# The output projection as seven half-block products: one change to a tuned transformer layer on one core

## The chip, the cores and the metric

The kernel runs on one core of one Trainium2 chip. The metric is device microseconds of one execution. A core has TensorE (PE in the profile, its weight loads PEld), VectorE (DVE), ScalarE (ACT), GpSimd (POOL) and SyncE (SP, which here only issues transfers). Every transfer is issued from the queue of SP, ACT or POOL and is carried by 16 DMA engines that all queues share.

## The reference

One layer of an image generator, 1024 latent tokens of 1024 features, 256 context tokens, all in float32:

```python
h = rmsnorm(x, norm_g) * (1 + scale) + shift          # scale, shift, gate from the condition c
q, k, v, za, u, bg, cg, zc = split(h @ w_in)          # eight groups of 512 columns
attn = neighbourhood_attention(q, k, v, kc, vc, rpb) * silu(za)   # 8 heads, 8x16 window + 256 context keys
conv = bg * conv3(cg * u) * silu(zc)
out  = x + gate * (concat([attn, conv]) @ w_out)      # (1024 x 1024) @ (1024 x 1024)
```

The change concerns the last line, the output projection: y = concat([attn, conv]) has 1024 tokens by 1024 features and w_out is 1024 by 1024.

## The kernel before

Every large product is made in three passes: each float32 operand is split into a high part, rounded to float32r by a cast on ACT, and a low part, which DVE makes by subtracting the high part. TensorE then sums high·high, high·low and low·high (`mm3`, lines 88 to 92). Everything before the last stage keeps this pattern:

- A prologue normalises and modulates x and leaves it as eight blocks `hh`, `hl` of 128 features by 1024 tokens.
- The projection loop (n from 0 to 34, 32 steps with a token tile each, four head pairs of eight tiles) makes q, k and v in `pacc`. While it works on one head pair, SP loads the eight weight chunks (`wr`) of the next one, ACT casts them and DVE makes their low parts `w`; four of the eight are split in the first step of the new pair. In this stage the order of PE, ACT, DVE, POOL and SP is the order of the code (`strict`). Weights, spilled q, k and v, and gate weights all pass SP's queue, in order.
- Attention runs in quarters (`quarter`), four for each of eight heads. Between the score products, products of other columns (`pu`) fill TensorE. SP loads k into a buffer tagged A and q into one tagged B, in the pool `hcp` for even heads. Each finished head pair is gated and its y block is written to DRAM (`y_d`).
- The output projection. `put_y(f)` loads feature block f of y (two transfers from ACT's queue) and splits it into `yh`, `yl`. `load_wo(nh, f)` loads the 128x512 block of w_out for feature block f and column half nh and splits it into `woh`, `wol`. Feature blocks come in the order `FORDER` = 4, 5, 6, 0, 1, 2, 3, 7, as they become ready. y is the stationary operand (128 tokens as columns), w_out the moving one (512 output columns). Eight token tiles by two column halves make 16 output tiles, each a sum of 8 blocks by 3 passes, 24 matmuls. Six tiles of the first half are summed together, block by block, then the remaining ten one after the other; the last one is made in two pieces of 384 and 128 columns. Feature block 3 is the last attention block; it is gated here, out of `z_d`, `o_d` and the reciprocal sums, which POOL loads (`rb`).
- The gate: for the first half of the columns the output tile is multiplied by the gate row on DVE (line 1343) and the residual x is added on POOL (line 1344); for the second half the gate is multiplied into w_out before the split (line 1288), and one DVE addition out of PSUM makes the result (line 1340).

In the stage after attention `strict` is empty: a scheduler in the compiler orders each engine's instructions by its own estimate of when they can start.

Of the kernel before, what the change touches and what calls it, by code (L numbers as in the profile page):

```python
# [10 lines left out]
F32 = mybir.dt.float32  # L11
# [44 lines left out]
def body(tc, es, x, xb, xt, cb_, ct, w_mod, w_gate, b_ada, w_grp, w_col, q_g, k_g, bias, w_out, vecs, cst, out):  # L56
# [47 lines left out]
    def many(name, n, shape):  # L104
        return [dr.tile(shape, F32, name=f"{name}{i}")[:] for i in range(n)]
# [11 lines left out]
    v_d = many("v_d", NPAIR, [P, 2, NB + 2, HD])  # L117
    kc_d = many("kc_d", NPAIR, [P, 2, L])
    ri_d = many("ri_d", NPAIR, [2, T])


    cp = es.enter_context(sbuf("cp"))
# [45 lines left out]
    hcs = ExitStack()  # L168
    hcp = hcs.enter_context(sbuf("hcp"))
    hc = []  # L170

# [224 lines left out]
    def blocked(v):  # L396
        return v.rearrange("p (b r c) -> p b r c", b=2, r=16)
# [716 lines left out]
    tiles, scales, waiting, nxt, raws = {}, {}, [], [], []  # L1114
    NT = NPAIR * NB

    def flush():
# [91 lines left out]
    vs_ = ExitStack()  # L1209
    prp = vs_.enter_context(sbuf("prp"))  # L1210
    vts = [prp.tile([P, NB + 2, HD], F32, name=f"v{i}") for i in range(2)]

    gating = []

# [27 lines left out]
    with sbuf("att") as ap, psum("psb") as psb:  # L1242
# [6 lines left out]
        for n in range(len(TICKS)):  # L1249
# [24 lines left out]
        strict[:] = []  # L1274
    vs_.close()
    prs.close()
    hcs.close()


    op = es.enter_context(sbuf("op"))  # L1280
    pss = es.enter_context(psum("pso"))
    y, wo = {}, {}

    def load_wo(wp, nh, f):
        raw = op.tile([P, 512], F32, name="woraw", tag="woraw", bufs=4)
        act.dma_start(raw, w_out[0, f * P:(f + 1) * P, nh * 512:(nh + 1) * 512])  # L1286
        if nh:
            dve.tensor_tensor(raw, raw, gate[:, 512:], ALU.mult)
        wh = wp.tile([P, 512], F32R, name=f"woh{nh}{f}")
        wl = wp.tile([P, 512], F32R, name=f"wol{nh}{f}")  # L1290
        act.copy(wh, raw)  # L1291
        dve.tensor_tensor(wl, raw, wh[:].bitcast(F32), ALU.subtract)  # L1292
        wo[nh, f] = wh, wl

    def put_y(yp, f):

        yh = yp.tile([P, T], F32R, name=f"yh{f}")
        yl = yp.tile([P, T], F32R, name=f"yl{f}")
        for half in range(2):
            cols = slice(half * 512, (half + 1) * 512)  # L1300
            tb = yp.tile([P, 512], F32, name="tb", tag="zt", bufs=4 if yp is op else 2)
            if f == NPAIR - 1:
                zs = op.tile([P, 512], F32, name="zs", tag="zt", bufs=4)
                rb = op.tile([P, 512], F32, name="rb", tag="rb", bufs=2)
                act.dma_start(zs, z_d[f][:, cols])
                act.dma_start(tb, o_d[f][:, cols])
                load_sums(f, half, rb, pool)
                act.activation(zs, zs, AF.Silu)
                dve.tensor_tensor(zs, zs, rb, ALU.mult)
                dve.tensor_tensor(tb, tb, zs, ALU.mult)  # L1310
            else:
                act.dma_start(tb, y_d[f][:, cols])  # L1312
            tv = blocked(tb[:]) if f < NPAIR else by_row(tb[:])
            act.copy(natural(yh[:], half), tv)  # L1314
            dve.tensor_tensor(natural(yl[:], half), tv, natural(yh[:].bitcast(F32), half), ALU.subtract)  # L1315
        y[f] = yh, yl

    for f in FORDER[:-1]:
        put_y(op, f)
        load_wo(op, 0, f)  # L1320
    load_wo(op, 0, FORDER[-1])
    hs.close()
    rp = es.enter_context(sbuf("rp", side="right"))
    put_y(rp, FORDER[-1])
    gate = rp.tile([P, D], F32, name="gate")
    sp.dma_start(gate, g_d.broadcast_to([P, D]))

    def out_mm(ps, nh, t, f, c=slice(0, 512)):
        rows = slice(t * P, (t + 1) * P)
        mm3(ps[:, c], y[f][0][:, rows], y[f][1][:, rows], *(w[:, c] for w in wo[nh, f]), f == FORDER[0], f == FORDER[-1])  # L1330

    def out_tile(ps, nh, t, pieces=(slice(0, 512),)):
        rows, cols = slice(t * P, (t + 1) * P), slice(nh * 512, (nh + 1) * 512)
        xr = rp.tile([P, 512], F32, name="xr", tag="xr", bufs=3)
        sp.dma_start(xr, x[0, rows, cols])
        ot = rp.tile([P, 512], F32, name="ot", tag="ot", bufs=3)
        if nh:
            for c in pieces:
                part = slice(c.start + 512, c.stop + 512)
                dve.tensor_tensor(ot[:, c], ps[c.start][:, c], xr[:, c], ALU.add)  # L1340
                sp.dma_start(out[0, rows, part], ot[:, c])
        else:
            dve.tensor_tensor(ot, ps, gate[:, cols], ALU.mult)
            pool.tensor_tensor(ot, ot, xr, ALU.add)
            sp.dma_start(out[0, rows, cols], ot)

    first = {t: bank("pout", "SCO"[t // 2]) for t in range(6)}
    for f in FORDER:
        for t in first:
            out_mm(first[t], 0, t, f)  # L1350
    for f in FORDER:
        load_wo(rp, 1, f)
    for t in first:
        out_tile(first[t], 0, t)
    for n, (nh, t) in enumerate([(0, 6), (0, 7)] + [(1, t) for t in range(NB)]):
        pieces = [slice(0, 384), slice(384, 512)] if (nh, t) == (1, NB - 1) else [slice(0, 512)]
        ps = {c.start: bank("pout", "USC"[(n + i) % 2 + i]) for i, c in enumerate(pieces)}
        for c in pieces:
            for f in FORDER:
                out_mm(ps[c.start], nh, t, f, c)  # L1360
        out_tile(ps if nh else ps[0], nh, t, pieces)


def constants():
# [58 lines left out]
```

## Time and profile before

| what | value |
|---|---|
| time, median of 3 runs | 607.62 us (606.13 to 609.37) |
| profiled execution, its own time | 607.57 us |
| span in its profile | 605.6 us |
| PE busy | 592.9 us, 98% |
| DVE busy | 399.7 us, 66% |
| ACT busy | 273.0 us, 45% |
| POOL busy | 66.3 us, 11% |
| first matmul of the output projection | 512.79 us |
| last DVE instruction | 602.73 us, for 0.29 us |
| mean granted TensorE clock | 0.994 |

In a timeline row stand the start, the duration, the engine, the line, the operation, what is written out of what, its shape, a count, and in brackets how long the engine was idle before and what ended that. Rows with a count stand for several instructions in a row. A tile row gives the shortest, median and longest duration in nanoseconds. A windows row gives, for a stretch, the busy time of each engine with its count, the granted clock, the busy share of the DMA engines and GB/s.

### The profile page before, as it was taken

How to read it: one execution, taken by the hardware profiler on the slowest of the kernel's cores; microseconds unless marked ns; L12 is line 12 of the kernel's file. 1: busy time of each engine (PE TensorE's matmuls, PEld its weight loads, DVE VectorE, ACT ScalarE, POOL GpSimd, SP SyncE). 2: the span in 40 equal slices, each digit the busy share in tenths (PEclk: the TensorE clock that was granted, in tenths of full speed). 3: DMA queues.
4: the chain of work that ended last, by engine and by line, in shares of the span. 5: the costliest groups of instructions: out<-in, count | busy, mean ns of one | idle time of the engine just before them, and what ended most of it. 6: DMA issues, size and time to landing. Idle time of an engine off the chain costs nothing. (4 is left out here: it accounts for less than half of the span.)

```text
span 605.6 us, 9468 instructions
## 1 busy us (share of the span) xinstructions
PE 592.9 (98%) x3347; PEld 502.0 (83%) x3348; DVE 399.7 (66%) x833; ACT 273.0 (45%) x636; POOL 66.3 (11%) x86
## 2 busy tenths in 40 slices
PE   7799999999999999999999999999999999999998
PEld 3477899999999999888878787877878777778887
DVE  1475889745636645458989697999798884394201
ACT  6645446426525445434554464646446444360000
POOL 1001025123223221100000000000000002003300
PEclk9899999999999999999999999999999999999999
DMA  8995566733524764766162838274823218963731
GB/s 331 412 416 201 179 214 188 254 126 114 191 91 148 225 222 162 280 237 217 52 246 93 275 106 297 94 264 155 307 87 92 89 36 238 332 195 105 244 106 52
DMA packets 63227, 116.14 MB, mean 192 GB/s; under 512 B 7377, under 2 KB 26313, under 8 KB 60876
## 3 DMA queue, kind: packets, MB, share of 16 engines
q1 hardware_dynamic: 57860, 105.82, 50.7%
q10 hardware_dynamic: 5064, 9.18, 4.8%
q0 software_dynamic: 256, 0.54, 0.3%
q8 instruction: 26, 0.43, 0.3%
q14 instruction: 21, 0.17, 0.1%
HBM read 86.08 MB, written 29.43 MB: 191 GB/s over the span
## 5 line engine op out<-in xcount | busy, mean ns | idle before, releaser
L71 PE MATMUL pu<-h,uh 128*128 128x512 f32 x544 | 172.2, 398 | 0.5 <-ACT zs L71 0.5
L71 PE MATMUL pacc<-w,h 128*128 128x384 f32 x768 | 138.8, 337 | 0.9 <-ACT ub L71 0.5
L71 PEld LDWEIGHTS pacc<-w,h 128*128 128x128 f32 x768 | 132.7, 188 | 1.8 <-ACT ub L71 0.9
L71 PEld LDWEIGHTS pu<-h,uh 128*128 128x128 f32 x544 | 97.2, 188 | 19.3 <-issue 1.2
L71 PE MATMUL pu<-h,ul 128*128 128x512 f32 x272 | 106.6, 392 | 0.0
L71 PEld LDWEIGHTS pu<-h,ul 128*128 128x128 f32 x272 | 51.1, 188 | 11.6 <-DVE ul L71 0.2
L71 POOL TENSOR_TENSOR ss<-ss,few 128x4 f32<-128x4 f32 (+1 forms) x40 | 41.1, 1028 | 126.3 <-DVE ss L71 126.1
L91 PE MATMUL pout<-wol,yh 128*128 128x512 f32 (+2 forms) x136 | 51.4, 379 | 0.0
L90 PE MATMUL pout<-woh,yh 128*128 128x512 f32 (+2 forms) x136 | 50.0, 381 | 0.5 <-ACT yh L1314 0.5
L92 PE MATMUL pout<-woh,yl 128*128 128x512 f32 (+2 forms) x136 | 49.3, 380 | 0.0
L71 PE MATMUL acc<-h,w 128*128 128x512 f32 x144 | 38.8, 415 | 0.0
L71 ACT ACTIVATE sc<-sc 128x512 f32<-128x512 f32 x32 | 20.2, 632 | 36.2 <-DVE sc L71 36.1
L71 DVE TENSOR_REDUCE ss<-sq 128x4 f32<-128x260 f32 (+1 forms) x40 | 15.7, 393 | 28.5 <-ACT sq L71 28.4
L71 PEld LDWEIGHTS acc<-h,w 128*128 128x128 f32 x144 | 26.9, 196 | 8.7 <-ACT h L71 1.2
L71 ACT COPY mg<-pmx 128x256 f32<-128x256 f32 (+1 forms) x33 | 12.1, 366 | 48.3 <-issue 22.8
L71 ACT ACTIVATE sq<-pacc 128x256 f32<-128x256 f32 x32 | 12.4, 387 | 47.4 <-PE pacc L71 46.7
L71 DVE TENSOR_TENSOR sum<-sum,sb 128x372 f32<-128x372 f32 (+2 forms) x64 | 31.0, 485 | 2.7
L71 ACT ACTIVATE qn<-pacc,ss 128x64 f32<-128x64 f32 x128 | 30.0, 330 | 4.9 <-PE trA L71 2.5
L71 DVE TENSOR_TENSOR mx<-mx,sb 128x372 f32<-128x372 f32 (+2 forms) x64 | 30.9, 483 | 1.9
L90 PEld LDWEIGHTS pout<-woh,yh 128*128 128x128 f32 x136 | 25.6, 188 | 5.9 <-ACT yh L1314 1.3
L71 DVE TENSOR_TENSOR sb<-pss,bt 128x192 f32<-128x192 f32 (+3 forms) x48 | 27.6, 601 | 4.2 <-PE pss L71 4.0
L92 PEld LDWEIGHTS pout<-woh,yl 128*128 128x128 f32 x136 | 25.6, 188 | 5.1 <-DVE yl L1315 0.4
(141 smaller groups left out, 931.1 us busy)
## 6 DMA issues: line engine op xcount, KB each, us to landing
uraw<-in_w_col SPq DMA_DIRECT2D x34, 256.0 KB, 2.9
slab<-in_w_mod SPq DMA_DIRECT2D x8, 1024.0 KB, 9.6
q_d<-qs SPq DMA_DIRECT2D x32, 256.0 KB, 2.0
k_s<-k_d SPq DMA_DIRECT2D x8, 1024.0 KB, 8.3
q_s<-q_d SPq DMA_DIRECT2D x16, 512.0 KB, 6.0
wr<-in_w_grp SPq DMA_DIRECT2D x40, 192.0 KB, 3.0
bt<-in_rpb SPq DMA_DIRECT2D x8, 564.0 KB, 6.2
xn<-in_xb SPq DMA_DIRECT2D x8, 512.0 KB, 8.1
```

Source lines behind the costliest of these rows:

```text
L71: i = emit(*a, **kw)
L90: i = pe.matmul(ps, ah, bh, start=first, stop=False)
L91: pe.matmul(ps, ah, bl, start=False, stop=False)
L92: pe.matmul(ps, al, bh, start=False, stop=last)
```

## The change

The output projection is computed transposed, output columns on partitions and tokens along the free axis, by a scheme of Strassen's kind with seven products of half blocks in place of eight. w_out is cut in four blocks of 512 features by 512 columns, with the feature blocks 4, 5, 6, 0 in the first half and 1, 2, 3, 7 in the second (`K_HALVES`); y is cut in four blocks of 512 features by 512 tokens. A product has four column tiles of 128x512, each a sum of 4 feature blocks by 3 passes: 48 matmuls. The left operand (stationary) is a block of w_out or a sum of blocks, the right one (moving) a block of y or a sum of blocks.

- Sums of w_out: steps 9, 13, 17 and 21 of the projection loop load two 128x1024 rows of blocks of w_out each, steps 11, 15, 19 and 23 combine them by four DVE operations and write the two sums to DRAM (`w_d`). They are read back later, as left operands of products 3, 5, 6 and 7; products 1, 2 and 4 take w_out itself.
- The left operands of products 1 and 5 are loaded during attention, into the buffers A and B of `hcp`, which now stays open; the others follow into A and B in turn.
- y blocks are loaded whole (512 KB a transfer). Sums of y blocks are made by DVE (`combined`, 16 operations). Every operand is split by one ACT cast and one DVE subtraction (`split`, 56 of each). Operand buffers exist for 8 right and 6 left operands in each of two pools.
- Sums of products are taken in PSUM: products 6, 7 and 4 go on in the banks `a` in which product 1 was left. What must be kept from `a` before that, and from product 5, is scaled by the gate into an SBUF tile by ACT (`pg`, three buffers) and added by POOL to a residual tile `m` (12 times each). All other results are added into `m` by DVE with the gate as a scalar (`gated_add`), and stored. The residual comes from the transposed x, 16 tiles of 256 KB.

```diff
-FORDER = [4, 5, 6, 0, 1, 2, 3, 7]
+K_HALVES = [4, 5, 6, 0], [1, 2, 3, 7]
...
+    def load_blocks(i):
+        for fs in K_HALVES:
+            wsum.append(bmp.tile([P, 3 * 384], F32, name="ws", tag="bt", bufs=2)[:, :D])
+            sp.dma_start(wsum[-1], w_out[0, fs[i] * P:(fs[i] + 1) * P])
+
+    def add_blocks(i):
+        (a11, a21), (a12, a22) = ([v[:, :512], v[:, 512:]] for v in wsum)
+        dve.tensor_tensor(a22, a21, a22, ALU.add)
+        dve.tensor_tensor(a21, a11, a21, ALU.subtract)
+        dve.tensor_tensor(a11, a22, a11, ALU.subtract)
+        dve.tensor_tensor(a12, a12, a11, ALU.subtract)
+        for k in range(2):
+            spill(w_d[i][:, k], wsum.pop(0))
...
+        if 9 <= n < 25 and n % 4 == 1:
+            load_blocks((n - 9) // 4)
...
         do_dves()
+        if 9 <= n < 25 and n % 4 == 3:
+            add_blocks((n - 9) // 4)
...
+    def load_left(q, tag):
+        left_raw[q] = hcp.tile([P, 4, 512], F32, name="wraw", tag=tag)
+        for i in range(4):
+            sp.dma_start(left_raw[q][:, i], left_rows(q, i))
...
+            if n in (30, 31):
+                load_left(*((1, "A"), (5, "B"))[n - 30])
             quarter(n)
...
+    def split(pl, name, bufs, v, view):
+        two = pl.tile([P, 2, 512], F32R, name=name, tag=name, bufs=bufs)
+        hi, lo = view(two[:, 0]), view(two[:, 1])
+        act.copy(hi, v)
+        dve.tensor_tensor(lo, v, hi.bitcast(F32), ALU.subtract)
+        return two[:, 0], two[:, 1]
+
+    def combined(dst, v, w):
+        dve.tensor_tensor(blocked(dst[:]), v, w, ALU.subtract)
+        return blocked(dst[:])
...
+    def prepare(q, pl):
+        for i in range(4):
+            right[q, i] = split(pl, "right", 8, right_side(q, i), blocked)
+            left[q, i] = split(pl, "left", 6, left_raw[q][:, i], lambda v: v)
+
+    def product(q, ps, tiles_, steps, first=False, cols=slice(0, 512)):
+        for i in steps:
+            for c in tiles_:
+                (ah, al), (bh, bl) = left[q, i], right[q, i]
+                at = slice(c * P, (c + 1) * P)
+                for n, (a, b) in enumerate(((ah, bh), (ah, bl), (al, bh))):
+                    pe.matmul(ps[c][:, cols], a[:, at], b[:, cols], start=first and i == 0 and n == 0,
+                              stop=i == 3 and n == 2, skip_group_check=True)
...
+    def gated_copy(ps, c, m):
+        pg = rp.tile([P, 512], F32, name="pg", tag="pg", bufs=3)
+        act.activation(pg, ps, AF.Identity, scale=gcol[:, c:c + 1])
+        pool.tensor_tensor(m, m, pg, ALU.add)
+
+    def gated_add(ps, c, m, cols=slice(0, 512)):
+        dve.scalar_tensor_tensor(m[:, cols], ps[:, cols], gcol[:, c:c + 1], m[:, cols], ALU.mult, ALU.add)
...
+    a = four("SSCC")
+    c5 = four("OOUU")
+    product(1, a, every_tile, range(4), first=True)
+    for c in every_tile:
+        product(5, c5, [c], range(4), first=True)
+    m11 = [residual(c, 0) for c in every_tile]
+    for c in every_tile:
+        gated_copy(a[c], c, m11[c])
+    load_left(2, "A")
+    prepare(2, rp)
+    m12 = [residual(c, 1) for c in every_tile]
+    m22 = [residual(4 + c, 1) for c in every_tile]
+    for c in every_tile:
+        gated_copy(c5[c], c, m12[c])
+        gated_copy(c5[c], 4 + c, m22[c])
+    c2_ = four("OOUU")
+    product(2, c2_, every_tile, range(4), first=True)
+    load_left(6, "B")
+    prepare(6, rp)
+    for c in every_tile:
+        product(6, a, [c], range(4))
+        gated_add(c2_[c], c, m11[c])
+        put(m11[c], c, 0)
...
```

After product 6 come product 3 (banks O and U again), 7 and 4 (banks `a`) in the same manner; the last tile of product 4 is made in pieces of 384 and 128 columns.

The new instructions stand in the engines' order as follows. On DVE, in the projection loop where one head pair ends and the next begins (`ws` are the rows of w_out, `w` the low parts of weight chunks):

```order
 L71 TENSOR_TENSOR rtmp<-qn,rope 128x256
 L71 TENSOR_TENSOR rot<-rot,rtmp 128x8x16 x2
+L71 TENSOR_TENSOR ws<-ws 128x512 x4
 L71 TENSOR_TENSOR w<-wr,w 128x384 x4
 L71 TENSOR_REDUCE ss<-sq 128x4
```

Four operations now stand ahead of the low parts of the next pair's last four chunks, here and at the next change of pair.

On DVE, in the output projection, before the change, where feature blocks 1, 2 and 7 of y and the second half of w_out are split:

```order
L1315 TENSOR_TENSOR yl1_5593<-tb_5594,yh1_5592 128x2x16x16
L1292 TENSOR_TENSOR wol07_5659<-woraw_5656,woh07_5658 128x512
L1288 TENSOR_TENSOR woraw_5831<-woraw_5831,gate_5679 128x512
L1315 TENSOR_TENSOR yl1_5593<-tb_5598,yh1_5592 128x2x16x16
L1315 TENSOR_TENSOR yl2_5609<-tb_5610,yh2_5608 128x2x16x16
L1292 TENSOR_TENSOR wol14_5835<-woraw_5831,woh14_5834 128x512
```

and with the change, up to the operands of product 6's third feature block (`right_5947`, `left_5950`; 5955 is the fourth block's; 6034 and 6040 belong to product 3, 6109 to 6133 to product 7, the `t` are sums of y blocks):

```order
L1350 TENSOR_TENSOR right_6040<-y7_5668,right_6040 128x512
L1354 TENSOR_TENSOR t3_6131<-y7_5668,y0_5587 128x512
L1350 TENSOR_TENSOR right_6109<-t3_6107,right_6109 128x512
L1350 TENSOR_TENSOR right_6117<-t3_6115,right_6117 128x512
L1350 TENSOR_TENSOR right_5947<-t2_5945,right_5947 128x512
L1350 TENSOR_TENSOR right_5955<-t2_5953,right_5955 128x512
L1350 TENSOR_TENSOR right_6125<-t3_6123,right_6125 128x512
L1354 TENSOR_TENSOR t2_5945<-y3_5649,t2_5945 128x512
L1350 TENSOR_TENSOR left_5950<-wraw_5924,left_5950 128x512
```

Between DVE's first operand (`left_5592`, the first row after the gating of the last convolution's first half) and `left_5950` stand 58 rows, all but one of them with two SBUF inputs.

On ACT, before the change, the output projection holds only loads and casts:

```order
L1291 CAST woh15_5841<-woraw_5838 128x512
L1308 ACTIVATE zs_5627<-zs_5627 128x512
L1291 CAST woh16_5848<-woraw_5845 128x512
L1286 DMA woraw_5866<-in_w_out 128x512
L1308 ACTIVATE zs_5639<-zs_5639 128x512
L1291 CAST woh10_5855<-woraw_5852 128x512
```

and with the change the scaled copies `pg` out of the banks of product 1 (5679 to 5682) and product 5 (5683 to 5686) stand between the casts:

```order
L1415 ACTIVATE pg_5851<-pout_5683,gcol_5677 128x512
L1415 ACTIVATE pg_5854<-pout_5684,gcol_5677 128x512
L1349 CAST right_6034<-y3_5649 128x512
L1349 CAST right_6040<-y7_5668 128x512
L1349 CAST right_6109<-t3_6107 128x512
L1349 CAST right_6117<-t3_6115 128x512
L1349 CAST right_5947<-t2_5945 128x512
L1415 ACTIVATE pg_5857<-pout_5684,gcol_5677 128x512
L1349 CAST right_5955<-t2_5953 128x512
L1349 CAST right_6125<-t3_6123 128x512
L1415 ACTIVATE pg_5860<-pout_5685,gcol_5677 128x512
L1349 CAST left_5950<-wraw_5924 128x512
```

`pg_5860` is the ninth of the twelve copies and stands one row ahead of the cast of `left_5950`; POOL's addition of each copy follows it.

More of the change, by code (lines that the diff above doesn't have):

```diff
@@ L1295, in put_y, with load_y @@
-    def put_y(yp, f):
-        yh = yp.tile([P, T], F32R, name=f"yh{f}")
-        yl = yp.tile([P, T], F32R, name=f"yl{f}")
+    raw_y, t1, t2 = {}, {}, {}
+    def load_y(f, queue):
+        raw_y[f] = op.tile([P, 2, 512], F32, name=f"y{f}")
+        if f != NPAIR - 1:
+            queue.dma_start(raw_y[f][:].rearrange("p a n -> p (a n)"), y_d[f])
+            return
         for half in range(2):
+            tb = raw_y[f][:, half]
             cols = slice(half * 512, (half + 1) * 512)
[L1301 to L1321, printed above, removed]
+            zs, rb = (op.tile([P, 512], F32, name=n, tag=n, bufs=1) for n in ("zs", "rb"))
+            queue.dma_start(zs, z_d[f][:, cols])
+            queue.dma_start(tb, o_d[f][:, cols])
+            load_sums(f, half, rb, pool)
+            act.activation(zs, zs, AF.Silu)
+            dve.tensor_tensor(zs, zs, rb, ALU.mult)
+            dve.tensor_tensor(tb, tb, zs, ALU.mult)
+    def y_block(k, i, half):
+        f = K_HALVES[k][i]
+        return (blocked if f < NPAIR else by_row)(raw_y[f][:, half])
@@ L1322, in body @@
+    for f in K_HALVES[0]:
+        load_y(f, act)
+    prepare(1, op)
+    prepare(5, op)
+    for f in K_HALVES[1]:
+        load_y(f, act)
     hs.close()
     rp = es.enter_context(sbuf("rp", side="right"))
[L1324 to L1361, printed above, removed]
+    gcol = rp.tile([P, KT], F32, name="gcol")
@@ new lines, in body, with residual @@
+    sp.dma_start(gcol, g_d.rearrange("o (t p) -> p (o t)", p=P))
+    every_tile = range(4)
+    def residual(c, half):
+        m = rp.tile([P, 512], F32, name="m", tag="m", bufs=14)
+        sp.dma_start(m, xt[c, :, half * 512:(half + 1) * 512])
+        return m
+    def gated_copy(ps, c, m):
[4 more added lines that the diff above has]
+        dve.scalar_tensor_tensor(m[:, cols], ps[:, cols], gcol[:, c:c + 1], m[:, cols], ALU.mult, ALU.add)
@@ new lines, in put, with four @@
+    def put(m, c, half, cols=slice(0, 512)):
+        sp.dma_start(out[c, :, half * 512 + cols.start:half * 512 + cols.stop], m[:, cols])
+    def four(tags):
+        return [bank("pout", tag) for tag in tags]
+    a = four("SSCC")
[7 more added lines that the diff above has]
+    load_left(2, "A")
@@ new lines, in body @@
+    prepare(3, op)
+    c3 = four("OOUU")
+    for c in every_tile:
+        product(3, c3, [c], range(4), first=True)
+        gated_add(a[c], c, m12[c])
+    load_left(7, "B")
+    prepare(7, op)
+    for c in every_tile:
+        product(7, a, [c], range(4))
+        gated_add(c3[c], c, m12[c])
+        put(m12[c], c, 1)
+    load_left(4, "A")
+    prepare(4, rp)
+    m21 = [residual(4 + c, 0) for c in every_tile]
+    for c in every_tile:
+        gated_add(a[c], 4 + c, m22[c])
+        put(m22[c], 4 + c, 1)
+        if c < 3:
+            product(4, a, [c], range(4))
+            gated_add(a[c], 4 + c, m21[c])
+            put(m21[c], 4 + c, 0)
@@ L1364, in constants @@
+    head_, tail = slice(0, 384), slice(384, 512)
+    last = {3: bank("pout", "O")}
+    gated_add(a[3], 7, m21[3], tail)
+    product(4, a, [3], range(4), cols=head_)
+    product(4, last, [3], range(4), first=True, cols=tail)
+    gated_add(a[3], 7, m21[3], head_)
+    put(m21[3], 7, 0, head_)
+    gated_add(last[3], 7, m21[3], tail)
+    put(m21[3], 7, 0, tail)
 def constants():
```

45 lines of the change are left out of this document (30 added, 15 removed).

## The prediction

> **What bounds the kernel now.** I read the page's engine totals first, then the windows of the last hundred microseconds, then the timelines of TensorE and VectorE there. The page and the windows:
>
> ```profile
> PE 592.9 (98%) x3347; PEld 502.0 (83%) x3348; DVE 399.7 (66%) x833; ACT 273.0 (45%) x636; POOL 66.3 (11%) x86
> ```
>
> ```profile
> 510.00:520.00 10.00, 10.00 (x46) 8.29 (x45) 5.13 (x9) 3.81 (x7) 2.07 (x4) 1.00 1.02 268
> 520.00:530.00 10.00, 9.77 (x42) 7.45 (x42) 3.28 (x5) 2.91 (x6) 0.00 (x0) 1.00 0.97 357
> 530.00:540.00 10.00, 9.78 (x44) 7.77 (x43) 8.89 (x15) 6.58 (x12) 0.00 (x0) 1.00 0.69 222
> 540.00:550.00 10.00, 10.00 (x46) 8.28 (x45) 8.84 (x15) 4.53 (x8) 0.00 (x0) 1.00 0.24 71
> 550.00:603.00 53.00, 52.69 (x251) 44.68 (x249) 11.18 (x17) 0.00 (x0) 10.24 (x8) 1.00 0.42 143
> ```
>
> TensorE is the bound throughout, at full clock; in the output projection it is never short of work for more than 0.23 us in ten. VectorE is busy at 0.9 only from 530 to 550 and hardly after. How long a matmul takes when nothing is missing is read from VectorE's last additions, each of which is released by the 24 matmuls of its tile:
>
> ```profile
> 590.48 0.69 DVE L1340 TENSOR_TENSOR ot<-pout,xr 128x512 f32<-128x512 f32 x1 [4.75 <-PE pout L92]
> 595.92 0.69 DVE L1340 TENSOR_TENSOR ot<-pout,xr 128x512 f32<-128x512 f32 x1 [4.75 <-PE pout L92]
> 600.10 0.56 DVE L1340 TENSOR_TENSOR ot<-pout,xr 128x384 f32<-128x384 f32 x1 [3.49 <-PE pout L92]
> 602.73 0.29 DVE L1340 TENSOR_TENSOR ot<-pout,xr 128x128 f32<-128x128 f32 x1 [2.07 <-PE pout L92]
> ```
>
> 595.92 - 590.48 = 5.44 us for 24, 0.2267 us each; 4.18 / 24 = 0.174 us at 384 columns and 2.63 / 24 = 0.110 us at 128. The stage begins here:
>
> ```profile
> 512.79 1.75 PE L90 MATMUL pout<-woh,yh 128*128 128x512 f32 x7
> ```
>
> **What the change removes.** Before: 15 tiles of 24 at 0.2267 (81.6 us) and the last one (6.8 us) make 88.4 us of the 89.9 us from 512.79 to 602.73; 1.5 us are waits for operands. After: seven products of 48 matmuls, 324 at 0.2267 (73.5 us), 12 at 0.174 and 12 at 0.110 (3.4 us), 76.9 us. So TensorE has 11.5 us less to do, and if the old 1.5 us of waits went too, 13.0 us. What follows the last matmul (an addition of 128 columns and its store) keeps its form. Everything else is the question of new waits, S.
>
> **What it adds ahead of the stage.** In the projection loop VectorE gets 16 operations, four at a time. Two groups stand right ahead of the low parts of the next pair's last four chunks:
>
> ```profile
> 162.65 0.49 DVE L71 TENSOR_TENSOR rot<-rot,rtmp 128x128 f32<-128x128 f32 x2
> 163.06 1.96 DVE L71 TENSOR_TENSOR w<-wr,w 128x384 fp32r<-128x384 f32 x4
> ...
> 204.86 1.96 DVE L71 TENSOR_TENSOR w<-wr,w 128x384 fp32r<-128x384 f32 x4
> ...
> 535.42 0.68 DVE L1315 TENSOR_TENSOR yl<-tb,yh 128x512 fp32r<-128x512 f32 x1
> ...
> 538.43 0.68 DVE L1288 TENSOR_TENSOR woraw<-woraw,gate 128x512 f32<-128x512 f32 x1
> ```
>
> ```profile
> 158.96 8.60 PE L71 MATMUL pacc<-w,h 128*128 128x384 f32 x48
> ```
>
> Operations of 128x512 without a wait between them follow each other every 0.602 us (five steps from 535.42 to 538.43). Four of them, 2.4 us, move the first of these low parts from 163.6 to 166.0. TensorE has two tiles from 158.96 on, 0.179 us a matmul; the second starts at 163.3 and asks for that low part with its 14th matmul, at 165.6. Wait: 0.4 us, the later chunks follow faster than they are used. The second change of pair has the same row at 204.86; 0.8 us in all. At steps 11 and 19 no such low parts stand behind the group and VectorE idles soon after; nothing.
>
> SP's queue gets 16 transfers of 512 KB. A store waits for VectorE, the next load for that store, and chunk loads stand behind both. The last ones of the pair:
>
> ```profile
> 155.12 2.50 SPq L71 DMA_DIRECT2D wr<-in_w_grp  x2
> ```
>
> ```profile
> 160.53 2.23 ACT L71 CAST w<-wr 128x384 fp32r<-128x384 f32 x5
> ```
>
> The last is issued at 157.6 and cast at about 162.2, and TensorE needs its chunk at 163.3 + 21 x 0.179 = 167.0, so some 4 to 5 us of lateness are covered by work that TensorE has; two transfers of 512 KB at 268 GB/s take 4 us. I take nothing; if that cover is used up, up to 5 us at each of two changes of pair (a rival). In attention, the eight loads of the first left operands (2 MB) go ahead of a weight load at 448.57 whose cast runs at 456.43:
>
> ```profile
> 448.57 0.33 SPq L319 DMA_DIRECT2D uraw<-in_w_col  x1
> ```
>
> ```profile
> 456.43 0.60 ACT L71 CAST uh<-uraw 128x512 fp32r<-128x512 f32 x1
> ```
>
> At 300 GB/s (between the windows above) 1.5 MB ahead of it take 5 us; it still arrives. Nothing, bounded by 2 us.
>
> **What it adds in the stage: VectorE.** From the end of the gating of the last convolution's first half, VectorE runs a queue without a gap:
>
> ```profile
> 507.55 0.69 DVE L71 TENSOR_TENSOR cv<-pu,cv 128x512 f32<-128x512 f32 x1 [1.47 <-PE pu L71]
> 508.16 1.28 DVE L1315 TENSOR_TENSOR yl<-tb,yh 128x512 fp32r<-128x512 f32 x2
> ```
>
> The first row that TensorE waits for, the low part of the first y block, is the ninth: 508.16 + 9 x 0.602 = 513.6, asked for at 513.7 (four high·high matmuls go first). [...] The tight one is `left_5950`, the 58th row: 508.16 + 58 x 0.602 = 543.1. TensorE asks for it after products 1 and 5, two blocks of product 6, two tiles of product 2 and 8 matmuls, 152 in all: 512.79 + 152 x 0.2267 = 547.3. So the queue is 4.2 us early, if nothing stops it. What it reads comes in time by the old rows; the slowest are the reciprocal sums of block 3:
>
> ```profile
> 510.06 2.07 POOL L530 DMA_DIRECT2D rb<-ri_d  x4 [4.86 <-PE pu L71]
> ```
>
> ```profile
> DMA to landing us min/median/max: 7.1/8.0/9.0
> ```
>
> Issued at 510.06, landed by 520, read by the 22nd row, at 508.16 + 21 x 0.602 = 520.8. Lateness up to the 4.2 us in hand costs nothing.
>
> **What can stop it: POOL.** Twelve additions of 128x512 on POOL, with both inputs in SBUF, now fall into this queue: they need product 1 (ends at 512.8 + 10.9 = 523.7) and the residual tiles, which SP issues behind a load that waits for VectorE's 23rd row, 522.0, so they begin at about 530. Ahead of `left_5950` on ACT stand nine of the scaled copies, with three buffers; at least six additions, likely nine, run before it. What such an addition does to VectorE, the trace shows for smaller ones in the projection loop:
>
> ```profile
> L71 DVE TENSOR_TENSOR rot<-rot,rtmp x64: 277/291/554, 88.8 to 256.4; 128x128 f32<-128x128 f32 x64
> ```
>
> ```profile
> L71 POOL TENSOR_TENSOR kn<-kn,gkc x8: 481/578/912, 98.5 to 222.2; 128x128 f32<-128x128 f32 x8
> ```
>
> ```profile
> 221.97 0.91 DVE L71 TENSOR_TENSOR rot<-rot,rtmp 128x128 f32<-128x128 f32 x2
> ```
>
> ```profile
> 221.78 0.95 POOL L71 TENSOR_TENSOR kn<-kn,gkc 128x128 f32<-128x128 f32 x2
> ```
>
> The pair of `rot` takes 0.49 us at 162.65 and 0.91 at 221.97, under two POOL multiplications; one goes from 277 to 554 ns. In the old output projection the same POOL addition did no harm, since VectorE read PSUM and one SBUF operand (0.69 us each, as without POOL):
>
> ```profile
> 551.94 2.05 DVE L1343 TENSOR_TENSOR ot<-pout,gate 128x512 f32<-128x512 f32 x3 [2.96 <-PE pout L92]
> ```
>
> ```profile
> 552.72 3.79 POOL L1344 TENSOR_TENSOR ot<-ot,xr 128x512 f32<-128x512 f32 x3 [40.60 <-DVE ot L1343]
> ```
>
> So VectorE with two SBUF operands loses 0.277 us to a POOL operation of 128 columns that takes 0.481. From 0.481 us (128 columns) and 3.79 / 3 = 1.26 (512), POOL needs 2.0 ns a column and 0.22 us besides; 128 columns are 0.26 us, about what VectorE lost. For 512 columns that is 1.04 us; the other bound is the whole operation, 1.26. Below, nothing, if POOL always finds VectorE waiting. [...] Nine of them: 10.8 us, less the 4.2 us in hand: 6.6 us of waiting on TensorE. Later queues (products 3, 7 and 4) have over 8 us in hand and are not reached.
>
> [...]
>
> **ACT and PSUM.** 56 casts at 0.52 and twelve copies at 0.6 make 36 us of the 76; ACT waits for POOL's buffers, not the reverse. Product 2's second tile needs the bank of product 5's second tile, so the 8th copy, so the 5th addition: 530 + 5 x (1.26 + 0.60), in turn with VectorE, is 539.3, asked for at 512.79 + 132 x 0.2267 = 542.7. Nothing beside the queue above, as long as POOL begins by 533.
>
> **The sum.** S = 0.3 + 6.6 + 0.8 = 7.7. The profiled execution, 607.57 us: 607.57 - 13.0 + 7.7 = 602.3. It lies 0.05 us from the median of the runs, 607.62, so I forecast **602.3 us**, 0.9% faster: about two fifths of the arithmetic's gain arrives. Differences within 0.5% (3.0 us) cannot be told from no change.
>
> **The rivals.**
>
> 1. *POOL does no harm*: its additions start late or fall into VectorE's waits. For it: the residual tiles are issued behind 0.5 MB of other loads, and the queue has 4.2 us in hand. Against: twelve additions of 1.26 us are 15 us, and VectorE has no wait of that length. S = 1.1, time 595.7.
> 2. *All twelve additions block VectorE for their whole length, and it alternates with them* (slower than before). Place: between product 5 and product 3. ACT's 4th to 9th copies then wait for POOL, the casts behind them come late, and VectorE waits for those casts in turn. [...] It decides from S = 13.0 on. Against: the 0.277 of the row above, which is less than the 0.481 of the whole operation.
> 3. *SP's order delays the weight chunks* in the projection loop: 2 to 5 us at each of two changes of pair on top of the forecast, 606.3 to 612.3, at 3.5 us each 609.3. For it: stores and loads that wait for each other. Against: the 4 to 5 us of cover.
>
> **Chances.** The forecast's case 0.45, its own range 599 to 606 (POOL's price 0.8 to 1.5 us each). Rival 1: 0.22, 595 to 599. Rival 2: 0.20, 606 to 612. Rival 3: 0.13, 605 to 611. The range that holds 8 in 10 reaches into both sides: 595.5 to 609.5. Faster by over 0.5% (below 604.6): most of the forecast's case and rival 1, 0.58; slower (above 610.7): parts of rivals 2 and 3, 0.11; within 0.5%: 0.31.
>
> **What would show it.** Right: about 348 matmuls of the output projection, 0.227 us apart inside a product; VectorE's operations around 530 to 550 much longer than 0.69 us wherever POOL's additions run, and these longer than 1.27; a gap of TensorE near the third block of product 6, released by DVE, 5 to 9 us with smaller ones before it. Rival 1: no gap above 1 us. Rival 2: gaps that go on past product 2, ACT idle before its copies with POOL as releaser. Rival 3: TensorE idle between 160 and 210. The forecast is wrong as a whole if TensorE's gaps come from transfers (y blocks, residual tiles), or if its matmuls are no longer 0.227 us apart.

## The result and the profile after

The changed kernel takes 610.01 us (median of 20 runs, 607.63 to 613.04); the kernel before, run beside it, 606.07 us (median of 20, 604.77 to 610.20). The ratio is 1.0055, 95% interval 1.0035 to 1.0074: slower by 0.55%, where 0.9% faster was forecast. The profiled execution took 613.04 us, the longest of the 20, with a span of 611.3 us.

TensorE's timeline of the changed kernel, from the first matmul of the output projection on (start, duration, count, and in brackets the idle time before it and what ended it):

```profile
520.37 30.25 PE L1390 MATMUL pout<-right,left 128*128 128x512 f32 x132
552.87 4.84 PE L1390 MATMUL pout<-right,left 128*128 128x512 f32 x13 [2.25 <-ACT pg L1415]
558.25 1.91 PE L1390 MATMUL pout<-right,left 128*128 128x512 f32 x7 [0.54 <-DVE right L1350]
563.89 44.26 PE L1390 MATMUL pout<-right,left 128*128 128x512 f32 x196 [3.74 <-DVE left L1350]
```

The stage takes 87.8 us (520.37 to 608.15) against 89.9 before; its arithmetic is 76.9. It has three gaps, 6.5 us together, and the third stands after 132 + 13 + 7 = 152 matmuls, where the forecast had put it. But 13 matmuls take 4.84 us, 0.37 each, where 132 without a gap take 0.229 each. The windows view of the same kernel says why (length, then busy time and count of PE, PEld, DVE, ACT and POOL, then the granted clock):

```profile
550.19:553.60 3.41, 1.16 (x5) 0.65 (x5) 3.41 (x6) 3.41 (x7) 1.17 (x2) 1.00 0.02 6
553.60:557.02 3.42, 3.42 (x9) 2.65 (x9) 3.42 (x4) 3.42 (x8) 2.84 (x2) 0.50 0.00 0
557.02:560.43 3.41, 2.59 (x10) 1.43 (x9) 3.41 (x5) 3.41 (x7) 1.76 (x2) 1.00 0.00 0
560.43:563.84 3.41, 0.00 (x0) 0.00 (x0) 3.41 (x4) 0.40 (x1) 2.86 (x2) 1.00 0.00 0
563.84:567.26 3.42, 3.37 (x8) 2.69 (x9) 3.42 (x6) 0.00 (x0) 0.00 (x0) 0.50 0.20 77
```

In the window after each of the two long gaps TensorE's granted clock is 0.50, for 3.42 us each time, and it loses 1.7 to 1.9 us more.

VectorE's timeline between 536 and 566, and POOL's:

```profile
536.19 2.51 DVE L1350 TENSOR_TENSOR left<-wraw,left 128x512 fp32r<-128x512 f32 x4
...
542.63 1.77 DVE L1354 TENSOR_TENSOR t<-y,t 128x512 f32<-128x512 f32 x1
544.33 1.77 DVE L1338 TENSOR_TENSOR zs<-zs,rb 128x512 f32<-128x512 f32 x1
546.02 1.77 DVE L1354 TENSOR_TENSOR t<-y,t 128x512 f32<-128x512 f32 x1
547.72 1.77 DVE L1339 TENSOR_TENSOR y<-y,zs 128x512 f32<-128x512 f32 x1
...
562.10 1.75 DVE L1350 TENSOR_TENSOR left<-wraw,left 128x512 fp32r<-128x512 f32 x1
```

```profile
537.79 12.86 POOL L1416 TENSOR_TENSOR m<-m,pg 128x512 f32<-128x512 f32 x7 [7.40 <-ACT pg L1415]
552.89 3.55 POOL L1416 TENSOR_TENSOR m<-m,pg 128x512 f32<-128x512 f32 x2 [2.24 <-ACT pg L1415]
557.68 1.67 POOL L1416 TENSOR_TENSOR m<-m,pg 128x512 f32<-128x512 f32 x1 [1.24 <-ACT pg L1415]
560.34 2.95 POOL L1416 TENSOR_TENSOR m<-m,pg 128x512 f32<-128x512 f32 x2 [0.99 <-ACT pg L1415]
```

While POOL adds, VectorE starts an operation every 1.70 us (542.63, 544.33, 546.02) in place of 0.60, so one addition costs it 1.10 us; POOL's own take 12.86 / 7 = 1.84 us in place of 1.26. Eleven of them run ahead of the `left` operand at 562.10, the one that ends the third gap, and the twelfth beside it (1.75 us): that operand is the 58th row, as forecast, its queue has no pause, and it ends at 563.85 in place of 515.74 + 58 x 0.602 = 550.7. The 13.2 us between are 12 x 1.10.

ACT's timeline shows the first gap's origin:

```profile
542.19 0.69 ACT L1415 ACTIVATE pg<-pout,gcol 128x512 f32<-128x512 f32 x1 [1.01 <-POOL m L1416]
...
549.53 1.14 ACT L1349 CAST right<-y 128x512 fp32r<-128x512 f32 x2 [3.25 <-DVE y L1339]
...
552.14 0.68 ACT L1415 ACTIVATE pg<-pout,gcol 128x512 f32<-128x512 f32 x1
```

The copy at 552.14 empties the PSUM bank for which TensorE waits. It stands on ACT behind casts that wait 3.25 us for VectorE's `y`, which is late by the same slow steps.

Ahead of the stage the time went here: in the projection loop (TensorE's, VectorE's and ACT's rows), and at the end of attention (VectorE, TensorE, POOL):

```profile
168.42 2.19 PE L71 MATMUL pacc<-w,h 128*128 128x384 f32 x11 [0.85 <-DVE w L71]
...
212.91 2.18 PE L71 MATMUL pacc<-w,h 128*128 128x384 f32 x11 [2.41 <-DVE w L71]
```

```profile
165.03 2.87 DVE L71 TENSOR_TENSOR ws<-ws 128x512 f32<-128x512 f32 x4
167.81 1.96 DVE L71 TENSOR_TENSOR w<-wr,w 128x384 fp32r<-128x384 f32 x4
```

```profile
207.03 0.37 ACT L71 CAST ks<-trB 128x256 fp32r<-128x256 f32 x1 [1.75 <-DMA k_d<-ks]
```

```profile
511.68 0.25 DVE L71 RECIPROCAL ri<-ri 128x16 f32<-128x16 f32 x1 [7.89 <-DMA ri<-rs_d]
```

```profile
512.53 0.50 PE L71 MATMUL pu<-h,ul 128*128 128x512 f32 x1 [1.64 <-DVE ul L71]
```

The two changes of pair wait for the low parts behind the sums, as forecast, but longer: the four sums take 0.695 us each (165.03 to 167.81), not 0.602, and at the second one ACT's casts of the chunks came late too, behind a cast that waited 1.75 us for a store of k to leave its buffer. From the first row of `pacc` to the last the loop takes 178.24 us (70.06 to 248.30); before, 174.42 (68.14 to 242.56). The two waits are 3.3 of these 3.8 us. At 512.53 TensorE waits 1.64 us for `ul`, which stands on VectorE behind the reciprocal of block 3's sums; their read landed late.

So the spans differ by 5.7 us: loop +3.8, `ul` +1.6, stage -2.1, its end +0.3, and +1.9 in the prologue, which the change doesn't touch. The rest is 0.2. The first row of `pacc` stood between 66.5 and 70.4 us in the twelve profiled executions of this study, whatever the kernel, and the granted clock of TensorE goes with it. Two windows of the prologue of the changed kernel:

```profile
7.47:10.88 3.41, 1.74 (x11) 0.98 (x10) 0.00 (x0) 2.50 (x5) 0.00 (x0) 1.00 0.98 400
10.88:21.12 10.24, 8.56 (x47) 3.52 (x47) 4.04 (x9) 2.78 (x7) 1.03 (x1) 0.50 1.03 417
```

Here the clock is halved for 10.24 us, as in the two other executions with a first row at 70.2 or later. It is halved for 6.83 us in the five with a first row from 67.5 to 69.4, the kernel before among them, and for 3.41 us or not at all in the four from 66.5 to 67.0. So these 1.9 us belong to the execution that was profiled and not to the change.

### The profile page after: what moved, and what is told of

Same layout as the page of the kernel before. It is cut to its first block, busy times and chain, and to the rows that moved or that the text cites. A ratio compares the mean times of both kernels' runs of the same rounds, so it can differ in the third digit from the quotient of the medians.

```text
span 611.3 us, 9489 instructions
## 1 busy us (share of the span) xinstructions
PE 586.5 (96%) x3287; PEld 493.4 (81%) x3288; DVE 445.6 (73%) x886; ACT 293.4 (48%) x672; POOL 76.9 (13%) x90
## 5 line engine op out<-in xcount | busy, mean ns | idle before, releaser
L1390 PE MATMUL pout<-right,left 128*128 128x512 f32 (+2 forms) x348 | 81.3, 396 | 6.5 <-DVE left L1350 3.7
L1390 PEld LDWEIGHTS pout<-right,left 128*128 128x128 f32 x348 | 66.4, 195 | 21.5 <-DVE left L1350 4.2
L71 PE MATMUL acc<-h,w 128*128 128x512 f32 x144 | 37.2, 403 | 1.2 <-ACT h L71 1.2
L71 ACT ACTIVATE sc<-sc 128x512 f32<-128x512 f32 x32 | 20.2, 632 | 36.6 <-DVE sc L71 36.6
L71 ACT ACTIVATE sq<-pacc 128x256 f32<-128x256 f32 x32 | 12.4, 387 | 48.7 <-PE pacc L71 45.9
L71 DVE TENSOR_TENSOR ul<-uraw,uh 128x512 fp32r<-128x512 f32 x34 | 23.0, 684 | 8.1 <-ACT uh L71 8.1
L1419 DVE SCALAR_TENSOR_TENSOR m<-pout,gcol,m 128x512 f32<-128x512 f32 (+2 forms) x22 | 15.0, 704 | 16.3 <-PE pout L1390 16.3
L71 DVE TENSOR_TENSOR sb<-sb,mg 128x744 f32<-128x744 f32 (+2 forms) x32 | 26.7, 834 | 0.0
```

Of the source, the lines that this page charges most:

```text
L71: i = emit(*a, **kw)
L1390: pe.matmul(ps[c][:, cols], a[:, at], b[:, cols], start=first and i == 0 and n == 0, stop=i == 3 and n == 2, skip_group_check=True)
L1419: dve.scalar_tensor_tensor(m[:, cols], ps[:, cols], gcol[:, c:c + 1], m[:, cols], ALU.mult, ALU.add)
```

## The experiments

Three theories of the stage were set against each other. A, the forecast's mechanism: an addition on POOL that reads SBUF takes time from VectorE, whose queue is full there. B: VectorE simply has too much to do. G: any operation on POOL there, with its waits and three buffers, holds ACT and VectorE up. The letters of the later runs (A and C to F) are explained in what was expected of each.

### The additions left out

```diff
     pg = rp.tile([P, 512], F32, name="pg", tag="pg", bufs=3)
     act.activation(pg, ps, AF.Identity, scale=gcol[:, c:c + 1])
-    pool.tensor_tensor(m, m, pg, ALU.add)
```

> The change without its twelve additions on POOL: the scaled copies are still made, but never added, so four products are missing from most of the output. Everything else is the same. Theory A: VectorE's steps stay at 0.60 us from 540 to 565, no gap of TensorE above 1 us in the output projection, its clock 1.00 throughout, so 6.5 + 3.8 us less than the change's 610.0: 600 us (598 to 602). Theory B: VectorE's queue is too long by itself; gaps remain, 606 to 610 us.

597.61 us (median of 4; 605.91 before beside it), ratio 0.9858 (0.9811 to 0.9905). The 348 matmuls run without a gap in 77.15 us, clock 1.00. B falls: without the additions the same work of VectorE is in time, though the scheduler put the `left` operand one row later (59th in place of 58th). 12.4 us less than the change's 610.01 is more than the gaps and the clock's fall in the output projection explain (87.8 - 77.15 = 10.7); the median of four runs leaves a microsecond or two.

### A fill, a copy in place of the addition

```diff
-    pool.tensor_tensor(m, m, pg, ALU.add)
+    pool.memset(pg, 0.0)           # the first run
+    pool.tensor_copy(m, pg)        # the second run
```

> The change with each of POOL's twelve additions replaced by a filling with zeros of the same scaled copy: POOL still waits for ACT's copy, still works on 128x512 and still gives the buffer back, but reads nothing; the sums of these products are left out of the computation. Theory A (VectorE loses time because POOL's addition reads its operands from SBUF while VectorE reads two): VectorE's steps stay at 0.60 us, no gap of TensorE above 1 us in the output projection, 597 to 600 us as without the additions. Theory G (any operation on POOL at that place, with its waits and the hand-over of the three buffers, holds ACT and VectorE up): gaps as in the change, 606 to 610 us.

> The change with each of POOL's twelve additions replaced by a copy of the scaled product over the residual tile: POOL reads one operand of 128x512 in place of two; the residual is left out of the sums. Theory A: reads of SBUF on POOL are what VectorE loses time to; a copy with half of them costs VectorE half of the 1.1 us or more, gaps of 1 to 4 us remain, 600 to 606 us. If only an operation with two SBUF inputs on both sides collides: no gap, 597 to 600 us. Theory G: 606 to 610 us.

The fill: 597.81 us, ratio 0.9864 (0.9845 to 0.9883). The copy: 598.93 us, ratio 0.9878 (0.9851 to 0.9904). TensorE, VectorE and POOL with the fill:

```profile
515.97 77.16 PE L1390 MATMUL pout<-right,left 128*128 128x512 f32 x348
```

```profile
536.27 0.68 DVE L1354 TENSOR_TENSOR t<-y,t 128x512 f32<-128x512 f32 x1
536.87 0.68 DVE L1338 TENSOR_TENSOR zs<-zs,rb 128x512 f32<-128x512 f32 x1
537.47 0.69 DVE L1354 TENSOR_TENSOR t<-y,t 128x512 f32<-128x512 f32 x1
```

```profile
536.71 3.42 POOL L1416 MEMSET pg<- 128x512 f32 x6 [1.61 <-ACT pg L1415]
```

and with the copy:

```profile
516.85 77.67 PE L1390 MATMUL pout<-right,left 128*128 128x512 f32 x348
```

```profile
537.74 1.09 DVE L1354 TENSOR_TENSOR t<-y,t 128x512 f32<-128x512 f32 x1
538.75 1.09 DVE L1338 TENSOR_TENSOR zs<-zs,rb 128x512 f32<-128x512 f32 x1
```

```profile
534.25 6.07 POOL L1416 COPY m<-pg 128x512 f32<-128x512 f32 x5 [7.38 <-ACT pg L1415]
```

The three VectorE operations are the same ones in the change and here. Their steps are 0.60 us beside POOL's fill, 1.01 beside its copy, 1.70 beside its addition: POOL's reads set the price, 0 for none, 0.41 us for one operand, 1.10 for two. G falls. The copy missed what A expected of it (1 to 4 us of gaps, 600 to 606 us), and its time lies where it was expected if only operations with two SBUF inputs on both sides collide; the steps of 1.01 us are what speaks against that. I had put its price at half of 1.1 us or more. At 0.41 all twelve are 4.9 us, little more than the queue's 4.2 us in hand; and the scheduler put the `left` operand 56th in this run, two rows earlier, so that the stage, 0.5 us longer than with the fill, does not test that sum.

### The additions kept, but late

```diff
-    pg = rp.tile([P, 512], F32, name="pg", tag="pg", bufs=3)
+    pg = rp.tile([P, 512], F32, name="pg", tag="pg", bufs=12)
     act.activation(pg, ps, AF.Identity, scale=gcol[:, c:c + 1])
-    pool.tensor_tensor(m, m, pg, ALU.add)
...
     product(6, a, [c], range(4))
-    gated_add(c2_[c], c, m11[c])
-    put(m11[c], c, 0)
+    gated_add(c2_[c], c, g11[c])
+    m = residual(c, 0)
+    pool.tensor_tensor(m, m, g11[c], ALU.add)
+    put(m, c, 0)
```

> The change with the same twelve additions on POOL, but each after the last product of its tile: twelve buffers for the scaled copies in place of three, VectorE adds the later products to these copies, and POOL adds the residual tile just before the store (residual tiles are loaded later, six buffers). The computation is complete. Theory A: the additions fall behind the stretch in which VectorE is full, ACT's copies wait for nobody; no gap of TensorE above 1 us from 550 to 565, clock 1.00 there, 600 to 603 us. Theory B: gaps as in the change, 608 to 610 us.

598.67 us, ratio 0.9880 (0.9832 to 0.9928), a complete computation with as many additions on POOL; no gap in the stage. VectorE and POOL:

```profile
558.15 4.01 DVE L1350 TENSOR_TENSOR left<-wraw,left 128x512 fp32r<-128x512 f32 x3
...
564.50 4.69 DVE L1422 SCALAR_TENSOR_TENSOR pg<-pout,gcol,pg 128x512 f32<-128x512 f32 x7
569.11 2.39 DVE L1350 TENSOR_TENSOR left<-wraw,left 128x512 fp32r<-128x512 f32 x2
```

```profile
555.78 5.23 POOL L1419 TENSOR_TENSOR m<-m,pg 128x512 f32<-128x512 f32 x3 [13.33 <-DVE pg L1422]
567.95 5.95 POOL L1419 TENSOR_TENSOR m<-m,pg 128x512 f32<-128x512 f32 x4 [6.93 <-DVE pg L1422]
```

The collision is still there: `left` with two operands in SBUF is stretched under both rows of POOL (4.01 us for three and 2.39 for two, where a single one takes 0.68). It falls where VectorE has time in hand. The operations that read PSUM and one SBUF operand (`pg<-pout,gcol,pg`) keep their 0.66 us: the seven from 564.50 on take 4.69 us, though POOL adds beside the last two of them, from 567.95 on.

### The additions on VectorE, out of PSUM

```diff
-    pg = rp.tile([P, 512], F32, name="pg", tag="pg", bufs=3)
-    act.activation(pg, ps, AF.Identity, scale=gcol[:, c:c + 1])
-    pool.tensor_tensor(m, m, pg, ALU.add)
+    dve.scalar_tensor_tensor(m, ps, gcol[:, c:c + 1], m, ALU.mult, ALU.add)
```

> The change, with its twelve additions on POOL and the twelve scaled copies on ACT replaced by twelve operations on VectorE that take the product from PSUM, scale it and add the residual tile (one operand in SBUF, 0.69 us each in the profile before). The computation is complete. Theory A (an addition on POOL costs VectorE's full queue 1.1 us, here 1.70 us a step in place of 0.60): the twelve cost 12 x 0.6 = 7.2 us of VectorE in place of 12 x 1.1 = 13.2, and ACT no longer waits for POOL; TensorE's gaps in the output projection fall from 6.5 us to 1 to 3 us, part of the 3.8 us lost at the lower clock goes too, time 602 to 606 us. Theory B (VectorE has too much to do there, and POOL is beside the point): VectorE gets 7 us more work, the gaps grow, 612 us or more.

598.96 us, ratio 0.9878 (0.9841 to 0.9915); no gap in the stage, though A expected 1 to 3 us.

```profile
540.50 2.71 DVE L1414 SCALAR_TENSOR_TENSOR m<-pout,gcol,m 128x512 f32<-128x512 f32 x4
...
546.91 3.69 DVE L1350 TENSOR_TENSOR left<-wraw,left 128x512 fp32r<-128x512 f32 x6
```

The twelve cost VectorE 0.66 us each, 7.9, as expected. What I had not expected is that the scheduler, with this other list of work, put six `left` operands at 546.91, ahead of sums and splits for later products that run before them in the change. That is argued from the two orders; no run holds the order fixed.

### The sums alone, and one step earlier

The first edit adds the loads, sums and stores of w_out's half blocks to the kernel before. The second moves them in the changed kernel:

```diff
-    if 9 <= n < 25 and n % 4 == 1:
-        load_blocks((n - 9) // 4)
+    if 8 <= n < 24 and n % 4 == 0:
+        load_blocks((n - 8) // 4)
...
-    if 9 <= n < 25 and n % 4 == 3:
-        add_blocks((n - 9) // 4)
+    if 8 <= n < 24 and n % 4 == 2:
+        add_blocks((n - 8) // 4)
```

> The kernel before with one part of the change alone: the loads, sums and stores of w_out's half blocks in the projection loop (their results are stored and not used; the computation is complete). Theory A (VectorE's four operations ahead of the next pair's low parts): TensorE waits at the two changes of pair, 0.8 to 1.3 and 0.8 to 2.4 us as in the runs so far, nothing elsewhere: 606.0 + 1.6 to 3.3 = 607.6 to 609.3. Theory D (the waits belong to the change as a whole, its other tiles and queues): no wait at 165 and 209, 606 us.

> The change with the sums of w_out's blocks, their loads and stores moved one step of the projection loop earlier (loads at steps 8, 12, 16, 20, sums at 10, 14, 18, 22), so that no group of four stands ahead of the low parts of the next pair's chunks. Theory A (these waits come from VectorE's four operations, 0.70 us each): the two waits of TensorE at 168 and 212 (0.85 and 2.41 us) go, 3.3 us less, 606.7 us. Theory C (they come from the transfers that the sums add to SP's queue, as the 1.75 us that ACT waited for the store of k at 207): the wait at 212 stays or moves to another change of pair, 608.5 to 610 us.

Alone: 608.32 us against 606.46 beside it, ratio 1.0035 (1.0019 to 1.0052), with these two waits:

```profile
164.88 2.20 PE L72 MATMUL pacc<-w,h 128*128 128x384 f32 x11 [0.82 <-DVE w L72]
```

```profile
208.19 2.21 PE L72 MATMUL pacc<-w,h 128*128 128x384 f32 x11 [1.25 <-DVE w L72]
```

One step earlier: 606.50 us, 3.5 us less than the change, ratio 1.0001 (0.9974 to 1.0029); neither wait is left, and the loop takes 174.44 us, as before the change, with as many loads and stores of 512 KB, a step earlier. So D falls, and C as it was put. The edit moves transfers and sums together and does not part them by itself: that VectorE's group ahead of the low parts costs some 0.8 us at each change of pair is read from the rows, where the low parts follow the sums without a pause; what comes on top, up to 1.6 us, goes with the store of k that holds up ACT's casts, and whether the added transfers delay that store was not taken apart. The loop took 176.6 to 178.2 us in all seven profiled runs with the sums at the old place.

Stalls of the output projection remain in that kernel, and in the window after the one with the least work of TensorE, 0.78 us, the granted clock is 0.50. Four windows of 3.41 us:

```profile
547.01:550.43 3.42, 1.62 (x8) 1.01 (x6) 3.42 (x4) 3.42 (x7) 2.23 (x3) 1.00 0.00 0
550.43:553.84 3.41, 1.91 (x7) 1.24 (x7) 3.41 (x4) 2.93 (x6) 2.47 (x2) 1.00 0.00 0
553.84:557.25 3.41, 0.78 (x3) 0.67 (x4) 3.41 (x4) 0.00 (x0) 2.02 (x2) 1.00 0.00 0
557.25:560.67 3.42, 3.42 (x9) 2.65 (x8) 3.42 (x7) 0.17 (x1) 0.00 (x0) 0.50 0.32 105
```

### Both together, and the read of the sums

> Both together: POOL's additions after the last product of each tile, and w_out's sums one step earlier. Theory A: the two effects add up; the stage runs without a gap (74.5 to 77 us) and the two waits of 0.8 us at the changes of pair go: 598.7 - 1.6 = 597.1 us (596 to 598.5). Theory E (one covers the other, since time won early is lost again at a later wait): 598.7 us.

> The twelve additions on VectorE from PSUM, and w_out's sums one step earlier. Theory A: 598.96 less the 0.80 and 1.05 us that TensorE waited at the changes of pair, 597.1 us. Theory E: 599 us.

595.52 us, ratio 0.9826 (0.9800 to 0.9853), with POOL's additions late; 595.71 us, ratio 0.9831 (0.9803 to 0.9858), with VectorE's. The effects add up (E falls), and by a microsecond and a half more than expected: of the 3.2 us, the loop's own length gives 2.2 (176.62 to 174.42); single times of these kernels lie between 594.7 and 599.0, so the rest is within what medians of four and six runs can tell. The prologue alone moves one execution by that much: the profiled one with POOL's additions late took 598.43 us, with the clock halved there for 10.24 us.

What is left is the wait for `ul`. POOL issues the read there; in the last run SP does:

```diff
-    pool.dma_start(ri, rs_d[p].rearrange("h b (x c) -> (h b x) c", c=16))
+    sp.dma_start(ri, rs_d[p].rearrange("h b (x c) -> (h b x) c", c=16))
```

> As the run with both together, and the read of block 3's sums (ri<-rs_d), for which VectorE's reciprocal waits, is issued by SP in place of POOL. Theory A: VectorE waits for this read with TensorE's next operand (ul) queued behind it, 1.1 to 1.6 us of TensorE; the change's larger loads ahead of it make it land 5 us after its issue where it took 3 before. If SP's read lands a microsecond or more earlier, TensorE's wait for ul goes: 596.0 us. Theory F (the transfers in flight hold it up whoever issues it): the wait stays, 597.1 us.

593.23 us, ratio 0.9788 (0.9764 to 0.9813): 2.1% faster than before, and 2.3 us less than both together, where the wait for `ul` is 1.1. The rest can't be put down to the read: the prologue alone moves single executions by as much (the first row of `pacc` stands at 67.90 in this profiled one, at 70.39 in that one). With POOL's read (the run with both together), its issue, VectorE, TensorE:

```profile
503.26 0.77 POOL L525 DMA_DIRECT2D ri<-rs_d  x1 [106.53 <-DMA rs_d<-sums]
```

```profile
507.69 0.25 DVE L71 RECIPROCAL ri<-ri 128x16 f32<-128x16 f32 x1 [7.40 <-DMA ri<-rs_d]
```

```profile
508.54 0.50 PE L71 MATMUL pu<-h,ul 128*128 128x512 f32 x1 [1.13 <-DVE ul L71]
```

and with SP's:

```profile
500.25 0.32 SPq L525 DMA_DIRECT2D ri<-rs_d  x1
```

```profile
502.17 0.25 DVE L71 RECIPROCAL ri<-ri 128x16 f32<-128x16 f32 x1 [4.36 <-DMA ri<-rs_d]
```

From issue to reciprocal 4.4 us with POOL, 1.9 with SP; TensorE's wait is gone (F falls). Before the change it was 3.1 us with POOL, and `ul` was in time. In flight beside POOL's read are the y blocks that ACT issues, now 512 KB each; that these made it slower is argued, no run took it apart.

## Why the prediction was wrong

- **The arithmetic held.** 76.9 us were forecast for the seven products; with no gap the stage takes 77.15 us.
- **The mechanism held, and its place**: VectorE with two SBUF operands loses time to POOL's additions, TensorE waits after the 152nd matmul, its releaser is `left`. POOL began 17.4 us after the stage's first matmul (537.79 - 520.37); 17.2 were forecast.
- **The step that failed first is "Nine of them: 10.8 us, less the 4.2 us in hand: 6.6 us of waiting on TensorE."** The price, 1.2 us, was near: no run shows a ground for 1.2 between the bounds of 1.04 and 1.26, and the steps of 1.70 us in place of 0.60 show 1.10. The number was not: all twelve ran before `left` was done, as the second rival had it. 12 x 1.10 - 4.2 = 9.0 us; TensorE asked at 520.37 + 152 x 0.2267 = 554.8 and got it at 563.9, 9.1 us later. My count took the order of ACT's copies ahead of the operand, and not that the slow steps themselves give POOL the time for the other three.
- **"Nothing beside the queue above, as long as POOL begins by 533" failed as well.** POOL began 17.4 us after the first matmul, where 20.2 were allowed, and the bank was late all the same. It is the 8th copy, as forecast, but that copy stands on ACT behind casts that wait for VectorE: I had asked when POOL begins, not what ACT's other rows wait for. Its gap (2.25 us) is part of the 9.1.
- **A term was missing: TensorE's clock.** 0.227 us a matmul was carried through the gaps. Behind two gaps stand two stretches at a granted clock of 0.50, 3.42 us each: 1.9 us within the 9.1, 1.9 after it. The forecast itself had said that it fails as a whole if the matmuls are no longer 0.227 us apart.
- **"0.8 us in all" for the changes of pair measured 3.8** in the profiled execution (2.2 to 3.8 over the runs). This is the largest single miss, 3.0 us. Two errors: 0.602 us a step where the sums take 0.695, and the cover of 4 to 5 us on SP's queue, which did not hold for ACT's casts at the second one.
- **"Nothing, bounded by 2 us" for the left operands' loads in attention held**: no wait of TensorE follows them. The 1.6 us at the end of attention had no term: I had taken the read of block 3's sums from the old rows ("What it reads comes in time by the old rows"), and it now lands late.

The terms as measured: 7.7 + 2.4 (three more additions, at 1.10) + 1.9 (clock after the last gap) + 3.0 (changes of pair) + 1.6 (`ul`) make S = 16.6 in place of 7.7, and 611.2 us in place of 602.3; with the prologue's 1.9 us that is 613.1, and the profiled execution took 613.04. The 0.3 us for the first operand of the stage did not come: no run shows the term, and no wait stands before 520.37; the end of the kernel took 0.3 more. The base of the forecast, 607.57 us, was itself one execution, 1.5 us above the median of the 20 runs. The second rival had the right count of additions and the right sign, and its range, 606 to 612 us, holds the median, but by terms that cancel: it took each addition at its whole length, 1.26 us where 1.10 was measured, and had no term for the clock. The third rival's place was right, the changes of pair; how much of the delay is the transfers', as it said, and how much VectorE's sums, no run took apart beyond the rows above. Moved by a step, neither costs anything.

## What to carry to other kernels

Before an elementwise operation goes to POOL, look at what VectorE does in the same microseconds: here POOL's 1.26 us cost VectorE 1.10 with two SBUF operands on both sides, and nothing where VectorE read PSUM; moving the same twelve operations behind the full stretch, or onto VectorE out of PSUM, was worth 11 us. Price a gap of TensorE with the clock that it may lose behind it (here 1.9 us behind each of two gaps, at a granted clock of 0.50), and count what else arrives while a slowed queue drains, not only what stands ahead of it now. In a stage whose order is fixed, put added VectorE work a step away from the operands that TensorE needs next.

## What the runs showed of the hardware

TensorE's granted clock fell to 0.50, for 3.41 us at a time in the output projection and for up to three times that (10.24 us) in the prologue, and in the changed kernel's execution the falls are a multiple of 3.41 us apart (553.60 and 563.84: three times 3.41; 10.88 and 553.60: 159 times). Cut into windows of that length and phase, the clock is 0.50 in the output projection (of the change, and of the change with its sums one step earlier) in the window after one in which TensorE was busy for 34%, 0% or 23% (1.16, 0.00 and 0.78 us), and it is 1.00 there and in the loop after windows with 47 to 56% (1.61 to 1.91 us). This is no threshold: in the prologue of the changed kernel it was 0.50 after a window with 1.74 us of TensorE (51%, the one from 7.47 above) and 1.00 after one with 1.53 (45%, from 24.54). What else decides, these traces do not show. After the gap of 2.25 us, which lies inside one window, the next window is at 0.50; the gap of 2.41 us before 212.91 lies across two windows of the same phase, and both are at 1.00 (the change's windows view):

```profile
208.86:212.27 3.41, 1.64 (x10) 1.32 (x8) 3.27 (x7) 1.89 (x8) 0.00 (x0) 1.00 0.65 249
212.27:215.68 3.41, 2.77 (x16) 2.69 (x17) 3.38 (x10) 0.54 (x2) 1.00 (x1) 1.00 0.97 353
```

The price that VectorE paid, with two SBUF operands of 128x512, went by what POOL read in these runs: 0 us beside the fill, 0.41 beside the copy with one operand of 128x512, 1.10 beside the addition with two, which took POOL 1.84 us there.
